# A hybrid decoder trunk: order of the first head's products, place of the residual-gate sums, evacuation of the delta gates

## The chip, the cores and the metric

The kernel runs on one core of a Trainium2 chip. The time is that of one execution on the device, in microseconds. A core has TensorE (PE, and PEld for its weight loads), VectorE (DVE), ScalarE (ACT), GpSimd (POOL) and SyncE (SP, whose queue here issues nearly all DMAs). Each works through its own queue in order and waits on semaphores of the others.

## The reference

One layer, sequence 1024, width 1024, float32:

```
shift, scale, gate = split(silu(c) @ ada_w + ada_b, 3)
h = rms_norm(x, norm_g) * (1 + scale) + shift
sq, sk, sv, sz, dq, dk, dv, dz, db, da, lq, lk, lv, lz, lr, mg = split(h @ w_in)
y_sb  = stick_breaking_attention(norm(q), norm(k), v) * silu(sz)      # 4 heads of 128
beta  = sigmoid(db);  g = -exp(a_log) * softplus(da + dt_bias)        # delta gates
y_gdn = rms_norm(gated_delta_rule(conv_silu(dq, dk, dv), beta, g)) * silu(dz)
y_gla = rms_norm(gla(lq, lk, lv, log_sigmoid(lr @ w2 + b) / 16)) * silu(lz)
merged = sum over the branches of sigmoid(mg) * (y_branch @ proj_branch)
out = x + gate * (merged @ w_out)                                     # residual gate
```

## The kernel before

Everything is kept transposed: channels on the 128 partitions, the 1024 tokens along a row. A float32 product is made of three: an operand is split into a high half (hi, rounded to fp32r) and the rest (lo), and hi x hi, hi x lo and lo x hi add up in one PSUM bank. `split` does it for a weight with a ScalarE cast (L157) and a VectorE subtraction (L158).

TensorE's instructions run in the order in which the program writes them. The other engines' instructions are put in order when the program is built, by a planner with its own estimates of time and with program order as priority. Tile pools give out a fixed number of buffers for each tag: 16 for "h" (the tiles of h and, at first, of ada), 8 for "raw" (weights as loaded), two PSUM banks for "acc", one for "tr".

**First head.** x is loaded, c is broadcast to all partitions and put through silu (`c_row`), and `rstd` comes out of sums of squares on TensorE. `keep_busy(5)` issues five products that nobody reads. Then a loop over the eight k tiles of h forms each tile and at once multiplies it with the first head's dq, dk, dv and dz weights. Four outputs (g) times two halves of the tokens (hf) take all eight PSUM banks, and a k tile makes 24 products. For each tile, `by_rows` (L374, L376) forms shift and scale: 128 rows of the transposed ada weight times `c_row`, summed along the row by VectorE, for the two of them. amp (L398) is (1 + scale) * norm_g; VectorE scales x with amp and rstd (L403), ScalarE adds shift and rounds to `hi` (L406), VectorE forms `lo` (L408). The loads of ada run three tiles ahead (`AHEAD`). Before, the 24 products go bank by bank:

```
for g in range(4):
    for hf in range(2):
        for n, (a, r) in enumerate(((0, hi), (0, lo), (1, hi))):
            mm(f_ps[g][hf], w[:, a, g, :], r[:, sl], 216, ...)
```

**Small projection and gates.** Then one group of 48 products (`run_cm`, two halves of 24, an acc bank each) projects lr, db and da together: rows 0 to 15, 32 to 35 and 64 to 67 of the output. `small_evac` copies it out with ScalarE (L503), GpSimd copies db (L504) and adds dt_bias to da (L505), and the lr rows go to DRAM. ScalarE forms sigmoid(db) (L515) and softplus(da) (L517 to L519), VectorE finishes and makes running sums by chunk (L520 to L526). The task `gates` (from L534) transposes these rows on TensorE into the one tr bank, four chunks at a time, and VectorE copies the bank into `beta_c` and `gam_c` (L542, L543); the second half needs the bank again.

**The rest.** `emit` writes TensorE's order by hand: it keeps a clock of planned matmul time (216 ns for a 512-wide product), and a task runs when its requirements are done and its lag in ns has passed; otherwise the next six products of the dense work (projections of later heads and merge gates, `run_cm`) are written. `gates` starts with a `yield 20400`. The tasks are the gated delta rule by head and half (G.a, G.b, G.v, G.s), GLA (L.w, L.p, L.s), attention (S.m) and, at the end of GLA, T.y, which loads y tiles into raw buffers and writes their differences. The task "cond" forms the residual gate: eight loads of 512 KB into the tags u6 and eight sums on VectorE (L314 to L318). Attention (`sb_mix`) runs roughly from 890 to 1150 us, merge and output projections after it. D.S2 is the end of the dense groups of the third attention head. The residual gate is read by the output projections alone.

Of the kernel before, what the change touches and what calls it, by code (L numbers as in the profile page):

```python
# [19 lines left out]
P = 128  # L20
D = 1024
# [31 lines left out]
def kernel(ctx: ExitStack, tc: tile.TileContext, xT: bass.AP, c: bass.AP,  # L53
# [258 lines left out]
    def conditioning(j, t_w="u6", t_p="u3"):  # L312
        aw = big(t_w)
        nc.sync.dma_start(out=aw, in_=adaT[j * P:(j + 1) * P, :])  # L314
        junk = big(t_p)
        nc.vector.tensor_tensor_reduce(out=junk, in0=aw, in1=c_row, scale=1.0, scalar=0.0,
                                       op0=ALU.mult, op1=ALU.add, accum_out=mod[:, j:j + 1])
        nc.vector.tensor_add(out=mod[:, j:j + 1], in0=mod[:, j:j + 1], in1=C("ada_b", j))  # L318
# [39 lines left out]
    keep_busy(5)  # L358
    AHEAD = 3

    def both(ap, k):
        return ap[:, k:k + 9:8]

    def conditioning2(k):
        tiles = [hp.tile([P, T], F32, tag="h", name="ada") for _ in range(2)]
        for i, t in enumerate(tiles):
            j = 8 * i + k
            nc.sync.dma_start(out=t, in_=adaT[j * P:(j + 1) * P, :])
        return lambda: by_rows(k, tiles)

    def by_rows(k, tiles):
        for i, t in enumerate(tiles):
            j = 8 * i + k
            nc.vector.tensor_tensor_reduce(out=t, in0=t, in1=c_row, scale=1.0, scalar=0.0,  # L374
                                           op0=ALU.mult, op1=ALU.add, accum_out=mod[:, j:j + 1])
        nc.vector.tensor_add(out=both(mod, k), in0=both(mod, k), in1=both(C("ada_b", 0, 24), k))  # L376


    first = (O_DQ, O_DK, O_DV, O_DZ)
    f_ps = [[None, None] for _ in first]  # L380
# [9 lines left out]
    for k in range(AHEAD):  # L390
        conds.append(conditioning2(k))
        if k < 3:
            raws.append(load_first(k))
    for k in range(KT):
        conds[k]()
        w = w_tile()
        split(w[:, 0], w[:, 1], raws[k])
        nc.vector.scalar_tensor_tensor(out=amp[:, k:k + 1], in0=mod[:, 8 + k:9 + k], scalar=1.0,  # L398
                                       in1=C("norm_g", k), op0=ALU.add, op1=ALU.mult)
        hi = hp.tile([P, T], F32R, tag="h", name="h_hi")  # L400
        lo = hp.tile([P, T], F32R, tag="h", name="h_lo")
        for sl in halves if k == 0 else (slice(0, T),):
# [4 lines left out]
                                 bias=mod[:, k:k + 1])  # L407
            nc.vector.scalar_tensor_tensor(out=lo[:, sl], in0=xs[k][:, sl],  # L408
# [9 lines left out]
        for g in range(4):  # L418
            for hf in range(2):
                if k == 0:  # L420
                    pool, tag = f_banks[2 * g + hf]
                    f_ps[g][hf] = bank(pool, tag, HALF)
                sl = slice(hf * HALF, (hf + 1) * HALF)
                for n, (a, r) in enumerate(((0, hi), (0, lo), (1, hi))):
# [74 lines left out]
    gt = [big("u7") for _ in range(2)]  # L499

    def small_evac(hf, sl, ps):
        raw = mid("v0")
        nc.scalar.copy(out=raw[0:96, :], in_=ps[0:96, :])  # L503
        nc.gpsimd.tensor_copy(out=rows[DB, sl], in_=raw[DB, :])  # L504
        nc.gpsimd.tensor_scalar(out=gt[0][DA, sl], in0=raw[DA, :], scalar1=C("dt_bias")[DA, :],  # L505
                                scalar2=None, op0=ALU.add)
        parts = [mid("v3", dt=F32R)[0:RANK, :] for _ in range(2)]
        split(*parts, raw[0:RANK, :])
# [5 lines left out]
    nc.scalar.activation(out=na[DA, :], in_=C("a_log")[DA, :], func=AF.Exp)  # L514
    nc.scalar.activation(out=rows[DB, :], in_=rows[DB, :], func=AF.Sigmoid)  # L515
    xg, sg = gt
    nc.scalar.activation(out=sg[DA, :], in_=xg[DA, :], func=AF.Abs)  # L517
    nc.scalar.activation(out=sg[DA, :], in_=sg[DA, :], func=AF.Exp, scale=-1.0)
    nc.scalar.activation(out=sg[DA, :], in_=sg[DA, :], func=AF.Ln, bias=one_c[DA, :])  # L519
# [1094 lines left out]
```

## Time and profile before

| | us |
|---|---|
| median of 3 runs | 1485.38 (1483.48 to 1486.11) |
| profiled execution | 1483.78 |
| its span | 1482.0 |

The span runs from the first to the last instruction that the profile shows; the rest of the execution's time lies around it. Times in the rows below are from the start of the span. An "idle before" is put down to the event that came last.

### The profile page before, as it was taken

The page shows a single profiled execution, that of the slowest core. Times are in us where ns is not written, and L with a number is a line of the kernel's source. Part 1 is how long each engine was busy: PE and PEld are TensorE (multiplying, and loading weights), DVE is VectorE, ACT ScalarE, POOL GpSimd, SP SyncE. Part 2 cuts the span into 40 slices and gives each one's busy share as a digit, 9 for nine tenths or more (in the row PEclk, how much of TensorE's full clock was granted, in tenths as well). Part 3 has the DMA queues.
Part 4 walks back from the last instruction along what each step waited for, and adds up shares of the span by engine and source line. Part 5 has one row for each costly group of instructions (what it writes and reads, how often), then busy time and mean ns, then how long its engine had stood idle before and what let it go on. Part 6 is the DMA issues. An engine that isn't in the chain of part 4 may idle for free.

```text
span 1482.0 us, 26690 instructions
## 1 busy us (share of the span) xinstructions
PE 1441.9 (97%) x10480; PEld 1206.6 (81%) x10480; DVE 918.8 (62%) x1914; ACT 697.9 (47%) x1470; POOL 151.5 (10%) x296
## 2 busy tenths in 40 slices
PE   7999999989999999999999999999999999999998
PEld 4877777877778887979788999899988888878777
DVE  7978647476643756667666535665566326589874
ACT  5367654453733747566486524342444434342321
POOL 1032232132321000000000100010000000000000
PEclk9999999999999999999999999999999999999999
DMA  9624332131321112121212132314223425474351
GB/s 351 183 78 118 102 88 62 44 92 42 104 86 40 41 51 66 35 60 35 73 47 54 55 107 72 100 43 147 60 86 108 142 85 171 139 244 129 119 175 61
DMA packets 174567, 144.31 MB, mean 97 GB/s; under 512 B 24773, under 2 KB 140613, under 8 KB 174442
## 3 DMA queue, kind: packets, MB, share of 16 engines
q1 hardware_dynamic: 174298, 142.30, 32.3%
q8 instruction: 82, 1.34, 0.4%
q14 instruction: 43, 0.35, 0.1%
q10 hardware_dynamic: 144, 0.31, 0.1%
HBM read 110.28 MB, written 32.29 MB: 96 GB/s over the span
## 4 chain that ended last, share of the span: by engine, by line
PE 76%; DVE 12%; DMA 4%; ACT 3%; POOL 2%; issue 2%; SPq 0%; DVEq 0%; POOLq 0%; ACTq 0%
PE acc L95 62%; PE lv L95 5%; PE mx L95 5%; PE tr L122 2%; DVE w L158 2%; DVE w L625 1%; DVE ada L374 1%; DVE w L623 1%; DVE u L435 1%; DMA v<-gam_d 1%; POOL c L301 1%; POOL u L505 1%; DVE u L403 1%; DVE h_lo L408 0%; ACT w L157 0%
## 5 line engine op out<-in xcount | busy, mean ns | idle before, releaser
L95 PE MATMUL acc<-h_hi,w 128*128 128x512 f32 x1856 | 653.4, 407 | 2.4 <-ACT u L295 2.0
L95 PEld LDWEIGHTS acc<-h_hi,w 128*128 128x128 f32 x1856 | 350.3, 189 | 73.8 <-ACT u L295 2.8
L95 PE MATMUL acc<-h_lo,w 128*128 128x512 f32 x928 | 364.1, 392 | 3.0 <-DVE h_lo L408 3.0
L157 ACT CAST w<-raw 128x512 fp32r<-128x512 f32 x232 | 141.8, 620 | 220.3 <-PE acc L95 192.0
L158 DVE TENSOR_TENSOR w<-raw,w 128x512 fp32r<-128x512 f32 x232 | 158.6, 691 | 129.4 <-ACT w L157 126.8
L95 PE MATMUL acc<-w,h_hi 128*128 128x256 f32 x1280 | 238.8, 287 | 0.0
L95 PEld LDWEIGHTS acc<-h_lo,w 128*128 128x128 f32 x928 | 175.9, 190 | 29.9 <-DVE h_lo L408 3.3
L95 PEld LDWEIGHTS acc<-w,h_hi 128*128 128x128 f32 x1280 | 198.8, 191 | 1.5 <-issue 0.7
L95 PE MATMUL acc<-w,h_lo 128*128 128x256 f32 x640 | 180.8, 282 | 0.0
L95 PE MATMUL acc<-u,w 128*128 128x512 f32 x744 | 180.0, 394 | 0.5 <-DVE v L1420 0.5
L95 PEld LDWEIGHTS acc<-u,w 128*128 128x128 f32 x744 | 139.5, 188 | 33.1 <-DVE v L1420 0.9
L95 PEld LDWEIGHTS acc<-w,h_lo 128*128 128x128 f32 x640 | 122.2, 191 | 0.0
L301 POOL TENSOR_TENSOR c<-c,mhalf 128x4 f32<-128x4 f32 (+1 forms) x56 | 54.9, 981 | 600.1 <-DVE c L299 575.7
L95 PE MATMUL acc<-unit,w 128*128 128x512 f32 x312 | 79.8, 393 | 1.1 <-DVE v L1475 1.1
L1224 ACT ACTIVATE v<-acc,col 128x512 f32<-128x512 f32 x48 | 33.0, 687 | 83.9 <-PE acc L95 83.4
L95 PEld LDWEIGHTS acc<-unit,w 128*128 128x128 f32 x312 | 58.4, 188 | 14.8 <-DVE v L1475 1.5
L1167 DVE TENSOR_TENSOR_SCAN u<-u,zero_c 128x128 f32<-128x128 f32 (+7 forms) x32 | 43.4, 1357 | 35.4 <-ACT u L1165 35.4
L95 PEld LDWEIGHTS mx<-r,u 128*128 128x128 f32 x288 | 44.2, 190 | 19.2 <-DVE r L804 5.2
L95 PE MATMUL mx<-r,u 128*128 128x128 f32 x288 | 48.3, 280 | 7.7 <-DVE r L804 2.8
L95 PE MATMUL lv<-u,u 128*32 128x32 f32 (+5 forms) x528 | 48.7, 250 | 2.2 <-DVE u L706 2.1
L95 PEld LDWEIGHTS lv<-u,u 128*32 128x32 f32 (+2 forms) x528 | 40.1, 145 | 11.2 <-issue 6.7
L295 ACT COPY u<-acc 128x512 f32<-128x512 f32 x50 | 29.1, 582 | 40.2 <-PE acc L95 39.6
(273 smaller groups left out, 1984.6 us busy)
## 6 DMA issues: line engine op xcount, KB each, us to landing
raw<-in_w_in SPq DMA_DIRECT2D x160, 256.0 KB, 3.1
g_dram<-v SPq DMA_DIRECT2D x48, 256.0 KB, 2.1
v<-g_dram SPq DMA_DIRECT2D x48, 256.0 KB, 2.9
ada<-in_adaT SPq DMA_DIRECT2D x16, 512.0 KB, 8.7
u<-in_xT SPq DMA_DIRECT2D x8, 512.0 KB, 7.6
u<-in_adaT SPq DMA_DIRECT2D x8, 512.0 KB, 3.7
v<-gam_d SPq DMA_DIRECT2D x16, 256.0 KB, 3.3
y_dram<-v SPq DMA_DIRECT2D x16, 256.0 KB, 2.1
```

The costliest lines, as they stand in the source:

```text
L95: return nc.tensor.matmul(out, lhsT=lhsT, rhs=rhs, **kw)
L122: nc.tensor.transpose(out=out, in_=in_, identity=ident[:k, :k])
L157: nc.scalar.copy(out=hi, in_=raw)
L158: nc.vector.tensor_sub(out=lo, in0=raw, in1=hi.bitcast(F32))
L295: nc.scalar.copy(out=dst[:, sl], in_=ps)
L301: nc.gpsimd.tensor_tensor(out=out, in0=out, in1=mhalf[:, 0:n], op=ALU.pow)
L374: nc.vector.tensor_tensor_reduce(out=t, in0=t, in1=c_row, scale=1.0, scalar=0.0, op0=ALU.mult, op1=ALU.add, accum_out=mod[:, j:j + 1])
L403: nc.vector.scalar_tensor_tensor(out=xs[k][:, sl], in0=xs[k][:, sl], scalar=amp[:, k:k + 1], in1=rstd[:, sl], op0=ALU.mult, op1=ALU.mult)
L435: nc.vector.scalar_tensor_tensor(out=t, in0=r[:, tap:tap + T], scalar=C("conv", j + tap), in1=t, op0=ALU.mult, op1=ALU.add)
L505: nc.gpsimd.tensor_scalar(out=gt[0][DA, sl], in0=raw[DA, :], scalar1=C("dt_bias")[DA, :], scalar2=None, op0=ALU.add)
L1167: nc.vector.tensor_tensor_scan(om[:, 0:n][:, ::-1], om[:, 0:n][:, ::-1], zero_c.broadcast_to([P, n]), 1.0, ALU.mult, ALU.add)
L1224: nc.scalar.activation(out=g, in_=ps, func=AF.Identity, bias=C("merge_b", gi * 8 + d))
```

## The change

- First head: for each k tile the 24 products run in the order high weight x hi (eight products, four outputs for each half of the tokens), low weight x hi (eight), high weight x lo (eight). `hi` of both halves is formed ahead of `lo`. One more warming product.
- The sums of k tiles 0 and 1 are formed together, ahead of amp for both; from then on one tile at a time. ada of tile 1 is loaded ahead of the first w tile. amp is formed in `by_rows`.
- c is written to DRAM once (4 KB). The task "cond" goes; a task T.c with the requirement D.S2 forms the residual gate in half rows: a broadcast of half of c into a raw buffer, eight loads of 256 KB into raw buffers and eight half sums, twice, 2500 ns of planned time between the steps. G.a no longer requires "cond", which had a lag of 1000 behind `gates`.
- Gates: ScalarE's evacuation adds dt_bias to all 96 rows (it is zero outside 64 to 67) and writes straight into `xg`; the two GpSimd instructions go, and sigmoid moves behind the softplus.

```diff
+    c_dram = dp.tile([1, T], F32, name="c_dram")
+    nc.sync.dma_start(out=c_dram, in_=c_row[0:1, :])
+
+    def gate_cond():
+        sums = cp.tile([P, 2, 8], F32, name="sums")
+        for hf, sl in enumerate(halves):
+            cr = flat(raw_tile())
+            nc.sync.dma_start(out=cr, in_=c_dram[:, sl].broadcast_to([P, HALF]))
+            for j in range(8):
+                aw = flat(raw_tile())
+                nc.sync.dma_start(out=aw, in_=adaT[(16 + j) * P:(17 + j) * P, sl])
+                yield 2500
+                nc.vector.tensor_tensor_reduce(out=aw, in0=aw, in1=cr, scale=1.0, scalar=0.0,
+                                               op0=ALU.mult, op1=ALU.add,
+                                               accum_out=sums[:, hf, j:j + 1])
+        nc.vector.tensor_add(out=sums[:, 0], in0=sums[:, 0], in1=sums[:, 1])
+        nc.vector.tensor_add(out=mod[:, 16:24], in0=sums[:, 0], in1=C("ada_b", 16, 8))
...
-    keep_busy(5)
+    keep_busy(6)
...
+    def by_rows(k0, n=1):
+        ks = slice(k0, k0 + n)
+        for k in range(k0, k0 + n):
+            for i, t in enumerate(conds[k]):
...
+        nc.vector.tensor_add(out=mod3[:, 0:2, ks], in0=mod3[:, 0:2, ks], in1=bias3[:, 0:2, ks])
+        nc.vector.scalar_tensor_tensor(out=amp[:, ks], in0=mod3[:, 1, ks], scalar=1.0,
+                                       in1=C("norm_g", k0, n), op0=ALU.add, op1=ALU.mult)
...
         conds.append(conditioning2(k))
-        if k < 3:
+        if k == 1:
+            raws.append(load_first(0))
+        if k:
             raws.append(load_first(k))
     for k in range(KT):
-        conds[k]()
+        if k != 1:
+            by_rows(k, 2 if k == 0 else 1)
...
-        for g in range(4):
-            for hf in range(2):
...
-                for n, (a, r) in enumerate(((0, hi), (0, lo), (1, hi))):
+        for n, (a, r) in enumerate(((0, hi), (1, hi), (0, lo))):
+            for hf, sl in enumerate(halves):
+                for g in range(4):
                     mm(f_ps[g][hf], w[:, a, g, :], r[:, sl], 216,
...
     def small_evac(hf, sl, ps):
-        raw = mid("v0")
-        nc.scalar.copy(out=raw[0:96, :], in_=ps[0:96, :])
-        nc.gpsimd.tensor_copy(out=rows[DB, sl], in_=raw[DB, :])
-        nc.gpsimd.tensor_scalar(out=gt[0][DA, sl], in0=raw[DA, :], scalar1=C("dt_bias")[DA, :],
-                                scalar2=None, op0=ALU.add)
+        nc.scalar.activation(out=xg[0:96, sl], in_=ps[0:96, :], func=AF.Identity,
+                             bias=C("dt_bias")[0:96, :])
...
-    tasks = [("gates", gates, [], 0), ("cond", gate_cond, ["gates"], 1000)]
+    tasks = [("gates", gates, [], 0)]
...
-                      ["gates", "cond", f"D.G{h}"] + prev(n, 1, "G.a") + prev(n, 3, "G.s"), 3000))
+                      ["gates", f"D.G{h}"] + prev(n, 1, "G.a") + prev(n, 3, "G.s"), 3000))
...
+    tasks.append(("T.c", gate_cond, ["D.S2"], 0))
```

## Rows read from the trace of the kernel before

**Rows 1.** Page, part 1: busy us, share of the span, instructions
```profile
PE 1441.9 (97%) x10480; PEld 1206.6 (81%) x10480; DVE 918.8 (62%) x1914; ACT 697.9 (47%) x1470; POOL 151.5 (10%) x296
```

**Rows 2.** The waits of TensorE, whole span: us in total, times, longest us
```profile
PE tr L122 <- DVE gam_c L543: 3.9, 1, 3.9
...
PE acc L95 <- DVE h_lo L408: 3.0, 1, 3.0
...
PE acc L95 <- ACT u L295: 2.0, 2, 1.6
```

**Rows 3.** Timeline of TensorE, 0 to 125 (start us, us, what, [idle before, releaser])
```profile
18.92 4.45 PE L95 MATMUL tr<-cst,ones 128*128 128x512 f32 x10
...
27.24 0.79 PE L95 MATMUL acc<-h_lo,w 128*128 128x512 f32 x1 [2.97 <-DVE h_lo L408]
...
35.25 0.39 PE L95 MATMUL acc<-h_hi,w 128*128 128x512 f32 x1
...
40.69 0.39 PE L95 MATMUL acc<-h_hi,w 128*128 128x512 f32 x1
...
73.33 0.39 PE L95 MATMUL acc<-h_hi,w 128*128 128x512 f32 x1
```

**Rows 4.** Timeline of VectorE, 14 to 62
```profile
17.18 1.22 DVE L374 CUSTOM_DVE_ANT_0 ada<-ada,u 128x1024 f32<-128x1024 f32 x1
...
22.21 0.75 DVE L403 SCALAR_TENSOR_TENSOR u<-u,amp,u 128x512 f32<-128x512 f32 x1 [2.28 <-ACT u L354]
...
40.51 1.29 DVE L403 SCALAR_TENSOR_TENSOR u<-u,amp,u 128x1024 f32<-128x1024 f32 x1
...
51.36 1.28 DVE L403 SCALAR_TENSOR_TENSOR u<-u,amp,u 128x1024 f32<-128x1024 f32 x1
```

**Rows 5.** Timeline of ScalarE, 60 to 145: the last h_hi
```profile
63.22 1.15 ACT L406 ACTIVATE h_hi<-u,mod 128x1024 fp32r<-128x1024 f32 x1
```

**Rows 6.** Timeline of GpSimd, 60 to 145
```profile
80.69 10.16 POOL L505 TENSOR_SCALAR u<-v,col 4x512 f32<-4x512 f32 x1
```

**Rows 7.** Timeline of ScalarE, 60 to 145: behind the gate rows
```profile
91.71 1.06 ACT L515 ACTIVATE u<-u 4x1024 f32<-4x1024 f32 x1 [4.38 <-POOL u L504]
92.79 1.28 ACT L442 ACT_TABLE_LOAD   x1
94.09 1.06 ACT L442 ACTIVATE u<-u 128x1024 f32<-128x1024 f32 x1
```

**Rows 8.** Timeline of VectorE, 60 to 145
```profile
106.55 2.62 DVE L526 TENSOR_TENSOR_SCAN u<-ones,u 4x128 f32<-4x128 f32 x8
...
112.20 1.22 DVE L316 CUSTOM_DVE_ANT_0 u<-u,u 128x1024 f32<-128x1024 f32 x1
...
114.02 0.17 DVE L542 COPY beta_c<-tr 128x16 f32<-128x16 f32 x1
```

**Rows 9.** Timeline of TensorE, 83 to 150
```profile
96.89 0.50 PE L95 MATMUL acc<-h_hi,w 128*128 128x512 f32 x1 [1.63 <-ACT u L295]
...
114.41 0.68 PE L122 MATMUL tr<-cst,u 128*128 128x128 f32 x4 [3.85 <-DVE gam_c L543]
114.80 0.73 PE L95 MATMUL acc<-h_hi,w 128*128 128x512 f32 x1
...
118.30 0.62 PE L95 MATMUL acc<-h_hi,w 128*128 128x512 f32 x2
```

**Rows 10.** Stretches of 10 us: busy us of each engine, granted clock, DMA share
```profile
90.00:100.00 10.00, 8.37 (x38) 6.59 (x37) 1.52 (x4) 8.14 (x9) 3.22 (x5) 1.00 0.47 129
```

**Rows 11.** Timeline of SP's DMA issues, 0 to 150
```profile
10.19 1.61 SPq L368 DMA_DIRECT2D ada<-in_adaT  x2
```

**Rows 12.** The tile ada: its loads from issue to landing
```profile
DMA to landing us min/median/max: 4.5/8.7/10.7
```

**Rows 13.** Stretches of 50 us: busy us of each engine
```profile
1000.00:1050.00 50.00, 50.00 (x360) 46.29 (x360) 26.39 (x37) 15.52 (x32) 0.00 (x0) 1.00 0.46 138
```

**Rows 14.** The page's DMA issues: KB each, median us to landing
```profile
raw<-in_w_in SPq DMA_DIRECT2D x160, 256.0 KB, 3.1
```

More of the change, by code (lines that the diff above doesn't have):

```diff
@@ L368, in conditioning2 @@
             nc.sync.dma_start(out=t, in_=adaT[j * P:(j + 1) * P, :])
[L369 to L380, printed above, removed]
+        return tiles
+    mod3, bias3 = (t.rearrange("p (i k) -> p i k", i=3) for t in (mod, C("ada_b", 0, 24)))
+    def by_rows(k0, n=1):
+        ks = slice(k0, k0 + n)
+        for k in range(k0, k0 + n):
+            for i, t in enumerate(conds[k]):
+                j = 8 * i + k
+                nc.vector.tensor_tensor_reduce(out=t, in0=t, in1=c_row, scale=1.0, scalar=0.0,
+                                               op0=ALU.mult, op1=ALU.add,
+                                               accum_out=mod[:, j:j + 1])
+        nc.vector.tensor_add(out=mod3[:, 0:2, ks], in0=mod3[:, 0:2, ks], in1=bias3[:, 0:2, ks])
+        nc.vector.scalar_tensor_tensor(out=amp[:, ks], in0=mod3[:, 1, ks], scalar=1.0,
+                                       in1=C("norm_g", k0, n), op0=ALU.add, op1=ALU.mult)
     f_banks = ((pa, "acc"), (pa, "acc"), (pm, "mx"), (pm, "mx"), (pt, "tr"), (pl, "lv"),
@@ L407 @@
                                  bias=mod[:, k:k + 1])
+        for sl in parts:
             nc.vector.scalar_tensor_tensor(out=lo[:, sl], in0=xs[k][:, sl],
@@ L417 @@
         h_lo.append(lo)
-        for g in range(4):
-            for hf in range(2):
[L420 to L423, printed above, removed]
-                for n, (a, r) in enumerate(((0, hi), (0, lo), (1, hi))):
+        if k == 0:
+            f_ps = [[bank(*f_banks[2 * g + hf], HALF) for hf in range(2)] for g in range(4)]
+        for n, (a, r) in enumerate(((0, hi), (1, hi), (0, lo))):
+            for hf, sl in enumerate(halves):
+                for g in range(4):
                     mm(f_ps[g][hf], w[:, a, g, :], r[:, sl], 216,
@@ L498 @@
     nc.gpsimd.memset(rows, 0.0)
-    gt = [big("u7") for _ in range(2)]
+    xg, sg = (big("u7") for _ in range(2))
     def small_evac(hf, sl, ps):
-        raw = mid("v0")
-        nc.scalar.copy(out=raw[0:96, :], in_=ps[0:96, :])
-        nc.gpsimd.tensor_copy(out=rows[DB, sl], in_=raw[DB, :])
-        nc.gpsimd.tensor_scalar(out=gt[0][DA, sl], in0=raw[DA, :], scalar1=C("dt_bias")[DA, :],
-                                scalar2=None, op0=ALU.add)
+        nc.scalar.activation(out=xg[0:96, sl], in_=ps[0:96, :], func=AF.Identity,
+                             bias=C("dt_bias")[0:96, :])
         parts = [mid("v3", dt=F32R)[0:RANK, :] for _ in range(2)]
-        split(*parts, raw[0:RANK, :])
+        split(*parts, xg[0:RANK, sl])
         for i, n in enumerate((0, 1, 0)):
@@ L513 @@
         pass
-    nc.scalar.activation(out=na[DA, :], in_=C("a_log")[DA, :], func=AF.Exp)
-    nc.scalar.activation(out=rows[DB, :], in_=rows[DB, :], func=AF.Sigmoid)
-    xg, sg = gt
     nc.scalar.activation(out=sg[DA, :], in_=xg[DA, :], func=AF.Abs)
     nc.scalar.activation(out=sg[DA, :], in_=sg[DA, :], func=AF.Exp, scale=-1.0)
+    nc.scalar.activation(out=na[DA, :], in_=C("a_log")[DA, :], func=AF.Exp)
     nc.scalar.activation(out=sg[DA, :], in_=sg[DA, :], func=AF.Ln, bias=one_c[DA, :])
+    nc.scalar.activation(out=rows[DB, :], in_=xg[DB, :], func=AF.Sigmoid)
     nc.vector.scalar_tensor_tensor(out=sg[DA, :], in0=xg[DA, :], scalar=0.0, in1=sg[DA, :],
@@ L1529 @@
                       [f"G.v{key}"] + prev(n, 1, "G.s"), 1050))
-    for n, (h, q) in enumerate(halves):
+    for n, (h, q) in enumerate(parts):
         g, key = L[h], f"{h}.{q}"
```

25 lines of the change are left out of this document (5 added, 20 removed).

## The prediction

> **What bounds the kernel now.** I read the busy shares first: TensorE is busy for 97% of the span [rows 1], so time comes back only where it idles or runs at its lower clock. The waits of TensorE rank the idling [rows 2]: the longest is the second transpose of the gate rows waiting for the copy into gam_c (3.9 us), then the first low product of the first head (3.0), and the two evacuations of an acc bank (2.0). All three lie in the first 120 us, which is where the change works. So the timeline of TensorE comes next, then those of the engines that it waits for.
>
> In the first head [rows 3], five warming products end at 18.92 + 4.45 = 23.37. One product follows, and then TensorE stands 2.97 us for h_lo of the first k tile. Once settled, a k tile takes 40.69 - 35.25 = 5.44 us for 24 products, 0.227 each. The small projection begins at 73.33. From 27.24 there are 191 products left, 43.3 us at the settled pace, and 46.1 passed: the other 2.8 us are products just after the wait at half the pace, the lower of the clock's two levels. VectorE is the close second: from one scaling of x to the one two tiles on, 51.36 - 40.51 = 10.85 us pass, 5.43 a tile [rows 4], with no idle between. It stood still only before 22.21, for 2.28 us, when the sums of tile 0 were done and rstd was not. The last h_hi starts at 63.22 and takes 1.15 [rows 5].
>
> The gates come next. GpSimd takes 10.16 us to add dt_bias to four rows [rows 6]. ScalarE, whose queue is in order, stands 4.38 us behind it with the sigmoid, then changes table at 1.28 us, and the evacuations queue behind [rows 7]; TensorE pays 1.63 us at 96.89 and the rest of the 2.0 at the next bank. The same lateness pushes the gate arithmetic on VectorE among the convolutions and the residual-gate sums: such a sum runs at 112.20, the copy of beta only at 114.02 [rows 8]. That holds the one tr bank, and TensorE stands 3.85 us until 114.41 [rows 9]. The eight products from 114.80 to 118.30 then take 3.5 us where 1.8 would do, half the pace again: 1.7 us more. In the ten microseconds that hold the 1.63 us gap the granted clock was 1.00 [rows 10], so a gap of that size cost its own length alone.
>
> **The change, part by part.** *High half first.* Of 24 products of a tile, 16 now need only h_hi, so h_lo may come 16 x 0.227 = 3.6 us after it. In the first tile h_lo came 2.97 us late, so the wait goes and, with it, the fall of the clock. The sixth warming product (0.89, from 4.45 / 5) ends at 24.3, and the first h_hi is there by then, since the one early product had ended at 27.24 - 2.97 = 24.27; it hides the start of the loop, and costs what the first product then begins late. 24.3 + 192 x 0.227 = 67.8, against 73.33: 5.5 us.
>
> *Sums of two tiles at once.* Four sums of 1.22 us from 17.18 end at 22.1, inside the 2.28 us that VectorE stood before rstd, so tile 1's two sums are free. Everything behind comes 2.3 us earlier; the last h_hi is ready near 63.22 + 1.15 - 2.3 = 62.1, and 5.44 us of products end at 67.5. The two bounds, 67.8 by TensorE and 67.5 by VectorE, meet, which is also the danger: neither has room. The sums need tile 1's rows of ada. They are now issued ahead of the first w tile; before they were issued from 10.19 to 11.80 [rows 11], and the slowest load of ada took 10.7 us [rows 12], so they might land at 22.5, the last sum end at 23.7 and amp be 1.8 us late. The ends are 3.7 and 5.5. The median landing of 8.7 is nearer to the good one; I take 5.0. The 4 KB write of c to DRAM stands in SP's queue, which would hold the loads behind it until c_row exists; xT still fills the queues then (SP is far ahead of what lands), so nothing.
>
> *One evacuation for the gates.* Adding dt_bias in ScalarE's evacuation removes two GpSimd copies and two additions, 10.16 us of them one after another on the chain. ScalarE then runs Abs, Exp, Ln and Sigmoid back to back, each 1.06 with a table change of 1.28: at most 4 x 2.34 = 9.4 us, and TensorE needs an acc bank again only 48 products (10.9 us) after the small projection. So the 2.0 us of bank waits go; the ends are 0 and 2.0, and I take 2.0. The gate rows are then ready some 14.5 us after the small projection (9.4, then VectorE's scans, 2.62, behind two steps of four rows that I estimate at the 1.22 of a sum), while the order written out for TensorE brings the transposes after 20.4. They were in time before too; what was late was the copy out of the bank. With the gate arithmetic earlier and the residual-gate sums gone from this stretch, VectorE has little ahead of the copies. I leave one convolution step of about the length of a sum (1.2) in the way in most outcomes. A gap as short as that did not lower the clock at 96.89. So of 3.85 + 1.7 = 5.5 us I take 4.5; the ends are 0 and 5.5.
> In the trace a table change is 1.28 us and the next instruction starts at 94.09, 0.02 us after its end [rows 7]. The Trainium skill (ScalarE: Activation LUTs, What ACT_TABLE_LOAD costs) has a drain of about 1.38 us on top. By it the chain would take an estimated 5.5 us more and use up nearly all the slack before the transposes; by the rows it doesn't.
>
> *Gate preparation starts 1 us sooner.* Without the task "cond" the first gdn_prep comes one step of six products (1.4 us) earlier, and all recurrences shift against the dense work. No row prices this: bounds -3 and +3, the size of the longest single waits [rows 2]; I take 0.
>
> *Residual-gate sums moved.* Eight loads of 512 KB and eight sums leave the stretch before 120. Into the attention stage go sixteen half sums, two broadcasts and sixteen loads of 256 KB through SP's queue. A half sum is about 0.6 us (half of 1.22), 10 us in all. From 1000 to 1050 TensorE is busy throughout, and VectorE 26.39 of 50 [rows 13]; it would rise to about 36. The cover is that slack; if it were gone, each half sum ahead of a weight split or a copy that feeds TensorE would cost 0.6. Bounds 0 and 5 (half of them); I take 0.5.
>
> **Sum.** 5.0 + 2.0 + 4.5 - 0.5 = 11.0 us. The profiled execution took 1483.78, span 1482.0 and 1.78 around it, which gives 1472.8. The median of the runs, 1485.38, lies 1.6 above it and would give 1474.4. I say 1474.
>
> **Rivals.** *The copies still come late.* VectorE's order is made when the program is built; if G.q's convolution again stands ahead of the copies, the 3.85 and 1.7 stay: 11.0 - 4.5 = 6.5 us, 1479. For it: the convolution steps are already interleaved with them. Against: they were there because the gate arithmetic came after 10 us of GpSimd.
>
> *VectorE or the loads set the first head.* If a k tile's h_hi is late by a sum (1.2) once or twice, 2.5 us of the 5.0 are lost: 1476.5. For it: 5.43 against 5.44.
>
> *Weight buffers run out in the attention stage.* This is the one that ends slower. The eight raw buffers now also hold a broadcast row and one or two ada pieces for sixteen steps of 2.5 us, some 40 us, during which about four weight groups of 10.9 us pass. If the next group's load has to queue behind an ada piece, TensorE waits out a whole landing, 3.1 us [rows 14], and 1.7 more at the lower clock: 4.8 each. From three groups on (14.4) it eats the gain; four (19.2) make 1493. For it: SP fills the buffers in order, and a piece is freed only when VectorE has summed it. Against: no TensorE wait at all in that stretch now.
>
> *Changing banks.* Each product now goes to another bank than the one before. The present kernel changes bank every third product and the pitch stays 0.227. If a change of bank made TensorE stutter until its clock fell for half of the 192 products, 96 x 0.22 = 21 us would be lost: 1495. It decides from 50 such products on (11 / 0.22).
> The Trainium skill (TensorE: Matmul & The Clock Gate, A second HAM failure mode: psum-queue depth-cycling) tells of such a kernel, cycling through banks with its clock swinging between its levels. The trace so far speaks against it.
>
> *It shifts and gives nothing.* The earlier recurrences meet new waits worth the whole gain: 1484. It would take four of the longest.
>
> **Chances.** Forecast 0.60, late copies 0.17, first head short 0.12, weight buffers 0.04, banks 0.03, nothing 0.04. About 0.2% (3 us) is what can be told from no change here. Forecast, late copies and short head are faster: 0.89. "Nothing" and a little of the buffers are the same: 0.05; the rest is slower: 0.06. The forecast's own range is 1469 (from 1483.78, every term at its good end and 2 from the shift) to 1477 (from 1485.38, the first head at 3.7 and 1.3 less elsewhere); an end at 1480.5 takes in both smaller gains, so 1469 to 1480.5 leaves out under 2 in 10.
>
> **What would show it.** Right: products from 24.3 on without a gap and at the high clock, the small projection starting near 68; no addition by GpSimd; no wait of TensorE for L295 near 90; the second gate transpose following the first at once near 102, without products at half pace; no wait of TensorE between 990 and 1060. Wrong: a gap before the second tile's first product, the copy of gam_c behind convolution steps, SP waiting on a raw buffer while TensorE waits for a split.

## The result, and the profile after

The changed kernel is slower: 1492.94 us median of four runs (1492.36 to 1496.05) against 1485.46 for the kernel before on the same chip, a ratio of 1.0056 to it (its 95% interval, here and below, in brackets: [1.0042, 1.007]). The forecast was 1474, with 1480.5 as its upper end, so it had the wrong sign. The profiled span is 1490.6, against 1482.0. One execution of single_sums below took 1747.11 us at a granted clock of 0.754 and isn't counted.

Part 1 of the page after, and its waits of TensorE over the whole span (us in total, times, longest), which answer to [rows 1, 2]:

```profile
PE 1446.5 (97%) x10482; PEld 1208.7 (81%) x10482; DVE 915.9 (61%) x1922; ACT 701.0 (47%) x1473; POOL 137.6 (9%) x292
```

```profile
PE mx L95 <- POOL u L784: 6.2, 2, 4.0
...
PE lv L95 <- ACT w L682: 3.1, 2, 2.3
...
PE tr L122 <- DVE u L1180: 2.3, 1, 2.3
...
PE acc L95 <- DVE v L1431: 1.8, 1, 1.8
...
PE tr L122 <- DVE gam_c L554: 1.5, 2, 0.8
```

The shares alone would say that little happened. The waits say that what was aimed at did go: no line of `h_lo`, none of the evacuation L295, and 1.5 us for gam_c in place of 3.9. Near the head of the list stand waits that belong to the gated delta stage (L784, L682) and to attention (L1180), where the change was not meant to act. (Lines after are those of before plus 11 from about L500 on: L784 was L773, L1240 was L1229.)

Where the time went is read by one comparison, used from here on: both kernels copy the same acc banks out of PSUM in the same order, so the start of the same copy in either trace tells how far one is ahead of the other. The copies taken are those at 79, 113, 199, 236, 336, 432, 914, 1006, 1057 and 1414 us of before. In the table, minus is earlier than before, in us:

| profiled run | 79 | 113 | 199 | 236 | 336 | 432 | 914 | 1006 | 1057 | 1414 |
|---|---|---|---|---|---|---|---|---|---|---|
| the change | -3.0 | -7.9 | -9.8 | -6.6 | -5.1 | -0.7 | -1.1 | -0.5 | 5.4 | 8.4 |

So up to 199 us the change earned 9.8 us, where the prediction's terms up to there make 11.5. The delta stage took 9 of them back by 432, attention cost 6 more between 1006 and 1057, and the merge the last 3. The merge's part is the wait for L1431 in the list above: VectorE, timeline 1316 to 1332, stood for the load of a merge gate (`g_dram`).

```profile
1321.76 0.69 DVE L1431 TENSOR_TENSOR v<-v,acc 128x512 f32<-128x512 f32 x1 [1.84 <-DMA v<-g_dram]
```

TensorE waited 1.76 us behind it (0.52 before), and its products from 1323.33 to 1326.31 were 0.43 apart, at half the pace. In no other profile is this wait longer than 0.95; whether it comes back in other executions of the change isn't shown.

**First head.** TensorE's timeline after, 18 to 72, and under it ScalarE's and VectorE's of the first 28 us (start, us, what, idle before), for [rows 3, 4]:

```profile
19.82 5.31 PE L95 MATMUL tr<-cst,ones 128*128 128x512 f32 x12
25.79 0.50 PE L95 MATMUL acc<-h_hi,w 128*128 128x512 f32 x1 [0.65 <-ACT h_hi L422]
...
43.14 0.50 PE L95 MATMUL acc<-h_hi,w 128*128 128x512 f32 x1 [0.73 <-ACT h_hi L422]
...
70.47 0.39 PE L95 MATMUL acc<-h_hi,w 128*128 128x512 f32 x1
```

```profile
25.01 1.39 ACT L422 ACTIVATE h_hi<-u,mod 128x512 fp32r<-128x512 f32 x2 [0.90 <-DVE u L419]
```

```profile
23.62 0.69 DVE L158 TENSOR_TENSOR w<-raw,w 128x512 fp32r<-128x512 f32 x1 [1.01 <-ACT w L157]
24.23 1.41 DVE L419 SCALAR_TENSOR_TENSOR u<-u,amp,u 128x512 f32<-128x512 f32 x2
```

The 2.97 us before the second product is gone, the clock stays at 1.00 (window 20 to 60), and the pitch is 0.227 with a change of bank at each product. The first product comes at 25.79, not 24.3: the warming products start at 19.82 where they started at 18.92 (x landed later in this execution, VectorE's first step on it starting at 8.01 for 7.65, as it did in a kernel that is the same as before up to there, see the end; the rest of the 0.9 wasn't followed), and VectorE, which had stood before rstd, now does the low half of the first weights ahead of the scaling of x. The small projection starts at 70.47 against 73.33.

**Gates.** TensorE's timeline, 94 to 125, for [rows 9]:

```profile
103.13 0.60 PE L122 MATMUL tr<-cst,u 128*128 128x128 f32 x4
105.94 0.63 PE L122 MATMUL tr<-cst,u 128*128 128x128 f32 x4 [0.83 <-DVE gam_c L554]
111.35 0.63 PE L122 MATMUL tr<-cst,u 128*128 128x128 f32 x4 [0.67 <-DVE gam_c L554]
```

Two waits of under 1 us in place of one of 3.85, and the products behind them keep the full pace.

**Delta stage.** The longest wait of the run, after: TensorE's timeline at 204 to 216, then ScalarE's and GpSimd's just ahead of it.

```profile
209.07 0.80 PE L95 MATMUL mx<-r,u 128*128 128x128 f32 x2 [4.02 <-POOL u L784]
209.51 0.77 PE L95 MATMUL acc<-h_hi,w 128*128 128x512 f32 x1
210.09 0.63 PE L95 MATMUL acc<-h_lo,w 128*128 128x512 f32 x1
```

```profile
201.61 1.28 ACT L1240 ACT_TABLE_LOAD   x1
202.90 0.63 ACT L1240 ACTIVATE v<-v 128x512 f32<-128x512 f32 x1
...
204.58 1.28 ACT L780 ACT_TABLE_LOAD   x1
205.88 1.28 ACT L780 ACTIVATE v<-v,gneg_c 128x128 f32<-128x128 f32 x4
207.06 0.61 ACT L783 ACTIVATE v<-v 128x512 f32<-128x512 f32 x1
```

```profile
207.75 1.26 POOL L784 TENSOR_TENSOR u<-u,v 128x512 f32<-128x512 f32 x1 [1.85 <-ACT v L783]
```

And the same places in the trace of before, ScalarE and then TensorE:

```profile
214.95 0.63 ACT L772 ACTIVATE v<-v 128x512 f32<-128x512 f32 x1
215.66 1.28 ACT L769 ACTIVATE v<-v,gneg_c 128x128 f32<-128x128 f32 x4
```

```profile
218.12 0.49 PE L95 MATMUL mx<-r,u 128*128 128x128 f32 x2 [2.11 <-POOL u L773]
...
218.69 0.40 PE L95 MATMUL acc<-h_lo,w 128*128 128x512 f32 x1
218.92 0.63 PE L95 MATMUL acc<-h_hi,w 128*128 128x512 f32 x2
```

TensorE needs `qd` (the line writes `mx`), GpSimd makes it from exp(gb), and ScalarE makes that. Before, ScalarE did exp(gb) first and the four other exps behind it. After, a sigmoid of a merge gate (L1240) stands between two groups of exps and costs two table changes of 1.28, and exp(gb) comes last. The wait grows from 2.11 to 4.02 us, and only behind the longer one do the products run 0.43 to 0.58 apart, at half the pace; the clock of the stretch says the same:

```profile
205.00:215.00 10.00, 5.98 (x22) 4.95 (x21) 6.12 (x21) 4.38 (x10) 3.43 (x4) 0.66 0.24 66
...
1000.00:1050.00 50.00, 47.03 (x334) 43.48 (x334) 31.00 (x58) 12.77 (x27) 0.00 (x0) 0.97 0.60 190
```

The last line is the attention stretch and answers to [rows 13]: 47.03 us of TensorE for 50.00.

### The profile page after: what moved, and what is told of

The parts are those of the page before. It is cut to its first block, busy times and chain, and to the rows that moved or that the text cites. A ratio compares the mean times of both kernels' runs of the same rounds, so it can differ in the third digit from the quotient of the medians.

```text
span 1490.6 us, 26720 instructions
## 1 busy us (share of the span) xinstructions
PE 1446.5 (97%) x10482; PEld 1208.7 (81%) x10482; DVE 915.9 (61%) x1922; ACT 701.0 (47%) x1473; POOL 137.6 (9%) x292
## 4 chain that ended last, share of the span: by engine, by line
PE 73%; DVE 10%; DMA 6%; ACT 5%; issue 2%; POOL 2%; SPq 1%; DVEq 0%; POOLq 0%; ACTq 0%
PE acc L95 60%; PE mx L95 6%; PE lv L95 5%; PE tr L122 2%; DVE u L450 2%; DVE w L158 1%; DMA v<-gam_d 1%; POOL c L301 1%; DMA raw<-in_adaT 1%; DVE w L634 1%; DVE w L636 1%; DMA u<-in_xT 1%; DMA u<-y_dram 1%; DMA raw<-y_dram 1%; ACT w L157 1%
## 5 line engine op out<-in xcount | busy, mean ns | idle before, releaser
L95 PEld LDWEIGHTS acc<-unit,w 128*128 128x128 f32 x312 | 58.4, 188 | 15.2 <-DVE v L1486 1.5
L295 ACT COPY u<-acc 128x512 f32<-128x512 f32 x50 | 29.1, 582 | 37.1 <-PE acc L95 36.9
```

The source lines that it names most:

```text
L95: return nc.tensor.matmul(out, lhsT=lhsT, rhs=rhs, **kw)
L295: nc.scalar.copy(out=dst[:, sl], in_=ps)
```

## The experiments

Theories for the delta stage. *Shift*: the gate preparation starts one step sooner and runs into work that isn't ready. *Queues*: the planner draws the orders of VectorE, ScalarE and GpSimd anew, and the draw of before was a good one. In the first expectations any new build does that; from lag_longer on, only moving the gate preparation, either way, does. *Chain*: the early gains are lost anyway. For attention: *Buffers* (the loads of the residual gate stand in SP's queue for raw buffers) against *VectorE* (the half sums themselves). The kernel before had a median between 1483.97 and 1486.83 on the chips used, so each kernel is told with its ratio to before on its own chip. The same copies as above, in the profiled runs (one execution each):

| profiled run | 79 | 113 | 199 | 236 | 336 | 432 | 914 | 1006 | 1057 | 1414 |
|---|---|---|---|---|---|---|---|---|---|---|
| lag_kept | -3.6 | -8.5 | -9.4 | -10.2 | -8.0 | -8.4 | -8.8 | -7.9 | -1.4 | -1.7 |
| sums_early | -2.7 | -7.0 | -6.9 | -7.5 | -7.9 | -8.4 | -8.7 | -8.1 | -7.1 | -6.8 |
| sums_late_alone | 2.0 | -0.9 | -3.1 | -3.9 | -1.2 | -1.5 | -1.9 | -1.6 | 4.5 | 5.0 |
| lag_alone | 0.9 | 0.9 | 4.0 | 6.5 | 9.2 | 12.5 | 12.1 | 12.4 | 12.4 | 12.9 |
| first_head_alone | -2.9 | -3.5 | 1.1 | 2.0 | 0.4 | 0.4 | 0.0 | 0.2 | 0.2 | 0.1 |
| gates_alone | 1.1 | -3.9 | -5.9 | -6.6 | -7.7 | -8.0 | -8.4 | -8.1 | -8.1 | -8.1 |
| sums_in_gla | -2.8 | -7.7 | -8.7 | -9.5 | -9.9 | -9.9 | -8.5 | -8.1 | -8.1 | -7.5 |
| sums_in_gla_again | -2.7 | -7.6 | -8.3 | -7.6 | -7.6 | -7.4 | -6.0 | -5.7 | -5.8 | -5.5 |
| lag_longer | -3.0 | -7.9 | -3.0 | -4.1 | 6.2 | 3.5 | 3.8 | 4.3 | 4.5 | 4.0 |
| lag_two_longer | -2.6 | -7.3 | -3.7 | -5.5 | 3.5 | 1.5 | 1.8 | 2.2 | 2.2 | 2.5 |
| single_sums | -1.8 | -5.3 | -2.5 | -3.3 | -5.0 | -4.6 | -4.9 | -4.4 | -3.6 | -3.3 |
| sums_own_buffers | 5.6 | 1.7 | 5.0 | 4.2 | 6.5 | 6.2 | 5.8 | 6.1 | 6.1 | 5.7 |
| loads_without_sums | -3.1 | -8.0 | -9.3 | -10.0 | -8.5 | -8.5 | -8.9 | -8.2 | 0.4 | -0.1 |
| sums_without_loads | -3.4 | -8.3 | -9.3 | -10.0 | -11.5 | -11.8 | -12.1 | -11.5 | -8.3 | -8.3 |

The two rows of sums_in_gla are one kernel, and differ by up to 2.5 us; so a difference of that size between two rows is not read as the work of an edit.

**lag_kept** puts the lag back by an empty task that does nothing:

```diff
+    def nothing():
+        return
+        yield
-    tasks = [("gates", gates, [], 0)]
+    tasks = [("gates", gates, [], 0), ("cond", nothing, ["gates"], 1000)]
-                      ["gates", f"D.G{h}"] + prev(n, 1, "G.a") + ...
+                      ["gates", "cond", f"D.G{h}"] + prev(n, 1, "G.a") + ...
```

> The changed kernel with an empty task in the place of cond, so that the first gdn_prep keeps its old lag and TensorE's order after the first head is that of the kernel before. Theory Shift (the one step by which gdn_prep moved forward costs the 9 us that the changed kernel gives back between 200 and 480 us): the lead of about 10 us at 199 us is still there at 480, the attention stage then takes its 6 us and the merge 2.7, about 1484. Theory Queues (the other engines' orders, planned anew at every build, cost it): part of the lead is lost although TensorE's order is the old one, 1486 to 1491. Theory Chain (the recurrences are bound by their own latency and cannot start earlier with profit): all of the lead is lost by 480, about 1493 as in the changed kernel.

Measured: 1480.09 us, ratio 0.9974 [0.9964, 0.9985]. From 113 to 432 the lead goes from -8.5 to -8.4, where that of the change fell from -7.9 to -0.7: the loss of the delta stage hangs on that one step. No theory had this time: Shift said 1484, Queues 1486 and more, and Queues in its first form falls, since a new build kept the lead. Most of the lead then goes in attention, from -7.9 to -1.4.

**sums_early** has the first head and the gates of the change, and the task "cond" with its eight whole sums as before.

```diff
-    tasks = [("gates", gates, [], 0)]
+    tasks = [("gates", gates, [], 0), ("cond", gate_cond, ["gates"], 1000)]
...
-    tasks.append(("T.c", gate_cond, ["D.S2"], 0))
```

> The changed kernel with the residual-gate sums back in their old place and form, task cond included; first head and gates as changed. Shift: 1475 (the lead of 10 us kept to the end). Queues: some of the lead lost in the recurrence stage, 1476 to 1482, with waits on other lines than in the changed kernel. Chain: 1485, no gain. All three: no loss of 5 us between 1030 and 1060 us, since no gate sum stands there.

Measured: 1479.32 us, ratio 0.997 [0.996, 0.998], and 1.0 us lost in attention.

**sums_late_alone** is the kernel before with the empty task and T.c as in the change.

> The kernel before with only the residual-gate sums moved into the attention stage; an empty task keeps the lag of gdn_prep, so TensorE's order is that of before throughout. Theory Buffers (the half sums take raw buffers and SP's queue, and the weight loads come late): the time line is level with before up to 1030 us, loses 4 to 6 us by 1060, with TensorE idle and its clock down between 1040 and 1050; about 1490, up to 1493 if the merge loses too. Rival, VectorE alone (the 16 half sums delay its other work a little each): 1 to 2 us, 1487, and the weight loads are in time.

Measured: 1485.10 us, ratio 1.001 [0.9999, 1.0021]. It gains about 4 us where the sums left (from 2.0 at 79 to -1.9 at 914) and loses 6.1 where they went.

**lag_alone** is the kernel before with one word taken out:

```diff
-                      ["gates", "cond", f"D.G{h}"] + prev(n, 1, "G.a") + ...
+                      ["gates", f"D.G{h}"] + prev(n, 1, "G.a") + ...
```

> The kernel before with gdn_prep no longer behind cond (one name taken out of one list); cond itself stays. Shift: 5 to 9 us slower, 1490 to 1494, lost between 200 and 480 us. Queues: anything from 3 us faster to 4 us slower, 1482 to 1489. Chain: no change, 1485.

Measured: 1497.07 us, ratio 1.0089 [1.0074, 1.0104], 13.1 us above before, nearly all of it lost between 113 and 432. That is more than any theory said; Shift, with 5 to 9, is nearest. Its waits of TensorE from 120 to 440 us begin with the one for qd, 4.0 us long as in the changed kernel; the second, one line below, is 1.4 there:

```profile
PE mx L95 <- POOL u L773: 6.3, 2, 4.0
PE lv L95 <- POOL w L649: 5.2, 2, 3.7
```

Set side by side with the trace of before, place by place (source line, operation, tile names and shapes; table loads and accumulator reads left out), lag_alone has another instruction in 1284 of TensorE's 10480 places, 315 of VectorE's 1890, 88 of ScalarE's 1191 and 21 of GpSimd's 296, all between 120 and 417 us. In lag_kept and sums_early the orders of TensorE, ScalarE and GpSimd between 140 and 436 us are those of before; VectorE's differs in one instruction of 549 and in three.

**lag_longer** and **lag_two_longer** are sums_early with the first gate preparation one and two steps later than before, which Shift and Queues answer differently. Against sums_early:

```diff
-    tasks = [("gates", gates, [], 0), ("cond", gate_cond, ["gates"], 1000)]
+    tasks = [("gates", gates, [], 0), ("cond", gate_cond, ["gates"], 2300)]
```

(3600 in the second.)

> First head and gates of the change, residual-gate sums in their old place, but the first gate preparation one step of six products LATER than before (lag 2300 for 1000), where the change has it one step earlier. Theory Queues: each step, whichever way, makes the planner draw VectorE's, ScalarE's and GpSimd's order in the delta stage anew, and the order of the kernel before is a lucky one; the draw costs some 5 to 12 us: median 1485 to 1491, with new waits of TensorE for GpSimd or ScalarE between 150 and 400. Rival Shift: only an earlier start is bad, because the recurrences then run into work that isn't ready; a later start costs at most its own 1.4 us: median 1479 to 1481.

> First head and gates of the change, residual-gate sums in their old place, the first gate preparation two steps later than before (lag 3600 for 1000). Theory Queues: a third draw of the orders in the delta stage; the lead of 7 to 8 us at 120 is lost again by 5 us or more before 430, median 1482 to 1492. Rival: one step either way was bad luck twice, and a draw is on average neutral: median 1477 to 1481.

Measured: 1488.87 us, ratio 1.0022 [1.0009, 1.0035], and 1484.6 us, 0.9994 [0.9982, 1.0006]. Both arrive at 113 with the lead of sums_early (-7.9 and -7.3) and lose 11.4 and 8.8 us of it by 432. Their own delay is 1.4 and 2.8. By the medians, against that of sums_early, they cost 9.1 and 3.6. Shift falls: later is bad too. Each draw has long waits of its own, again behind engines that are fed in a new order; the first line of each list:

```profile
PE lv L95 <- DVE w L676: 6.0, 3, 2.9
```

```profile
PE lv L95 <- DVE u L706: 4.8, 1, 4.8
```

But waiting is mostly the smaller part of the loss. Below is the stretch between the copies at 113 and 432 of before, in each kernel's own trace: before, the change, lag_alone, lag_longer, lag_two_longer (busy us of TensorE, its weight loads, VectorE, ScalarE and GpSimd, then the granted clock).

```profile
113.00:432.00 319.00, 301.98 (x2467) 243.23 (x2468) 202.22 (x614) 176.44 (x433) 92.29 (x188) 0.99 0.30 82
...
105.00:431.00 326.00, 304.68 (x2465) 244.43 (x2465) 197.09 (x606) 180.14 (x435) 90.58 (x187) 0.98 0.28 78
...
114.00:444.00 330.00, 308.66 (x2463) 247.44 (x2464) 200.38 (x614) 180.33 (x435) 91.69 (x188) 0.97 0.29 79
...
105.00:435.00 330.00, 308.52 (x2459) 247.25 (x2459) 201.16 (x615) 178.67 (x434) 89.79 (x188) 0.96 0.30 81
...
106.00:433.00 327.00, 308.75 (x2458) 247.93 (x2459) 200.09 (x615) 180.92 (x436) 91.22 (x188) 0.96 0.30 82
```

TensorE idles 17.0 us before and 18.3 to 21.5 in the four others; for the same products it is busy 2.7, 6.7, 6.5 and 6.8 us longer, as the granted clock falls. So in the last three most of the loss is products at half the pace, not waiting. (One execution each; the two profiles of sums_in_gla have a clock of 1.00 and 0.99 in this stretch.)

**first_head_alone** and **gates_alone** are the kernel before with one of the two groups of edits each.

> The kernel before with the first head's edits alone: order of the products, sums of tiles 0 and 1 together, sixth warming product. Theory Additive: the first head ends 2.9 us earlier, as in the changed kernel, and TensorE's later order is that of before, so the lead lasts: median about 3 us under the kernel before (2 to 4). The evacuation of the gates still goes over GpSimd, so the bank waits (2.0) and the late copy of gam_c (3.9) are there. Rival Chain: the gate rows set when the delta stage can run and GpSimd's 10 us are still in them; then the lead is used up by 130 us and the median is within 1 us of before. Rival Redrawn: moving VectorE's first instructions redraws its later order too and costs some microseconds, median 0 to 10 above before.

> The kernel before with the gates' edits alone: ScalarE's evacuation adds dt_bias, no GpSimd instructions, sigmoid last. TensorE's order is untouched. Theory Additive: first head and gates together led by 7 us, the first head by 2.9 of it; so the gates alone lead by about 4 us from 120 us on (bank waits 2.0 gone, wait for gam_c 3.9 down to about 1.5), median 3 to 5 under before. Rival: the copies are late because VectorE has the residual-gate sums and convolutions ahead of them; then only the bank waits go, median 1 to 2 under before.

Measured: 1483.66 us, ratio 0.999 [0.9977, 1.0003], and 1478.02 us, 0.9954 [0.9937, 0.9972]. Additive fails: the gates alone give all of it, the first head nothing that can be told from none. The first head's 3.5 us at 113 are gone at 199. In its trace, TensorE (first fence) and VectorE (second), and under them TensorE at the same place before:

```profile
168.25 1.08 PE L95 MATMUL lv<-u,u 64*64 64x64 f32 x8 [3.18 <-DVE u L710]
169.26 0.79 PE L95 MATMUL acc<-h_hi,w 128*128 128x512 f32 x1
```

```profile
163.02 0.17 DVE L627 TENSOR_TENSOR w<-w,w 32x15 f32<-32x15 f32 x1 [2.93 <-DMA w<-ad]
```

```profile
170.00 0.65 PE L95 MATMUL lv<-u,u 64*64 64x64 f32 x8 [0.96 <-DVE u L706]
```

TensorE got to this step of the inverse 4 us sooner. It waits for VectorE's copies L710 (L706 before), and ahead of those, in VectorE's in-order queue, stand steps of a gate preparation (L627) whose rows come back from DRAM (`ad`) only 2.2 us sooner than before. So TensorE waits 3.18 for 0.96 and runs at half pace behind it. That the recurrence doesn't come sooner with the dense products is what Chain said, with the loss some 50 us later than it put it. In gates_alone the recurrence moves and the lead grows from -3.9 to -8.0.

**single_sums** is sums_early with the first two tiles' sums one at a time again.

> First head and gates of the change, residual-gate sums in their old place, but the sums of k tiles 0 and 1 one tile at a time as before. Theory Pair sums matter: with single sums the first tile is ready 1.2 us sooner, yet VectorE is then 2.4 us behind for the later tiles and sets the first head: waits for h_hi between 30 and 70 and the small projection no sooner, median 0 to 2 above the kernel with pair sums (1479 to 1481). Rival: the pair sums only delay the first product (amp at 22.5, first product at 25.8 for 24.3 forecast); then single sums gain 1 us.

Measured: 1478.6 us (the four executions counted), ratio 0.9955 [0.9937, 0.9973]. The small projection is about 1 us later than with pair sums (-1.8 for -2.7), and at the end the two can't be told apart: one more sign that time won in the first head doesn't reach the end.

For attention, ScalarE, SP's issues and TensorE of lag_kept:

```profile
1031.72 0.62 ACT L1329 CAST u<-u 128x512 fp32r<-128x512 f32 x1 [4.32 <-DMA u<-y_dram]
...
1034.81 0.28 ACT L1176 ACTIVATE u<-lv 128x128 f32<-128x128 f32 x1
```

```profile
1027.02 0.33 SPq L323 DMA_DIRECT2D raw<-in_adaT  x1
...
1028.04 0.38 SPq L1328 DMA_DIRECT2D u<-y_dram  x1
```

```profile
1036.87 0.33 PE L122 MATMUL tr<-cst,u 128*128 128x128 f32 x1 [2.21 <-DVE u L1180]
1036.95 0.63 PE L95 MATMUL acc<-h_hi,w 128*128 128x512 f32 x1
1037.38 0.63 PE L95 MATMUL acc<-h_lo,w 128*128 128x512 f32 x1
```

and its list of SP's waits between 1000 and 1060:

```profile
SPq L323 <- DVE sums L325: 11.4, 8, 3.6
```

SP stands 11.4 us, in eight waits, until a half sum has given a raw buffer back for the next piece of ada. Behind it in the queue is a load of y_dram; ScalarE, in order, stands 4.32 us behind that load's cast, and behind the cast are the sigmoids (L1176) of the third attention head (an expectation below calls it the fourth). The scan and its product (L1180) follow on VectorE, from 1036.00 on, behind weight splits and a half sum at 1034.19; TensorE waits 2.21 us, and its next products are 0.43 apart.

**sums_own_buffers** is lag_kept with two buffers of their own and GpSimd's queue for the pieces (and for the two broadcasts).

```diff
-                aw = flat(raw_tile())
-                nc.sync.dma_start(out=aw, in_=adaT[...])
+                aw = wp.tile([P, HALF], F32, tag="own", name="own", bufs=2)
+                nc.gpsimd.dma_start(out=aw, in_=adaT[...])
```

> The changed kernel with the old lag kept and the residual-gate sums in attention as the change has them, but their tiles from two buffers of their own and their loads issued by GpSimd's queue. The half sums on VectorE stay where they were. Theory Queue of SP: nothing is then ahead of the y_dram loads and the weights in SP's queue, ScalarE's 4.32 us stand behind such a load goes, and the wait of 2.2 for the first transposes of the fourth head (L122) with it; attention costs under 1.5 us, median 7 to 9 under before (about 1476). Rival VectorE: the half sums themselves hold the scans and copies of attention; the 2.2 us wait and the half-pace products stay, and the median is 3 to 5 under before, as with the raw buffers.

Measured: 1489.55 us, ratio 1.0024 [1.0011, 1.0036], for another reason: with nothing to hold them, the planner spread the half sums from 23 to 158 us, two of them in the first head, where TensorE waited 7.7 us for one h_hi. It doesn't test what it was made for, since no half sum ran in attention.

**loads_without_sums** and **sums_without_loads** part the two, on lag_kept. The first sums 8 of 512 columns of each piece; the second does not load the pieces and multiplies constants in their place. Neither forms the residual gate.

```diff
-                nc.vector.tensor_tensor_reduce(out=aw, in0=aw, in1=cr, ...
+                nc.vector.tensor_tensor_reduce(out=aw[:, 0:8], in0=aw[:, 0:8], in1=cr[:, 0:8], ...
```

```diff
-                nc.sync.dma_start(out=aw, in_=adaT[(16 + j) * P:(17 + j) * P, sl])
-                nc.vector.tensor_tensor_reduce(out=aw, in0=aw, in1=cr, ...
+                nc.vector.tensor_tensor_reduce(out=aw, in0=cst[:, 0:HALF], in1=cr, ...
```

> The version with the old lag kept, residual-gate sums in attention, but each half sum over 8 of its 512 columns (so the residual gate is wrong); broadcasts and the sixteen loads of 256 KB stay. Theory Queue of SP: the loads are what costs; a load of y_dram still comes late, ScalarE stands 2 us or more behind it near 1030, and the lead that the profile has at 998 falls by 4 us or more to 1060. Rival VectorE: with the half sums gone the lead falls by less than 2 us.

> The same version, but the sixteen pieces of ada are not loaded: each half sum multiplies a half row of the constants with the broadcast of c and writes it into the raw buffer (so the residual gate is wrong); buffers and half sums stay, only two broadcasts are loaded. Theory Queue of SP: without the loads SP holds nothing back for long; the lead at 998 falls by less than 2 us to 1060. Rival VectorE: sixteen half sums of 0.69 us hold the scans and copies of attention; the lead falls by 4 us or more.

Measured: 1483.23 us, ratio 0.998 [0.997, 0.999], and 1478.38 us, 0.9949 [0.9931, 0.9967]. From 1006 to 1057 the first loses 8.6 us, the second 3.2, lag_kept 6.5. The first line of TensorE's waits from 990 to 1070, with loads and without:

```profile
PE tr L122 <- DVE u L1180: 4.5, 1, 4.5
```

```profile
PE tr L122 <- DVE u L1179: 2.5, 1, 2.5
```

The loads are the larger part, as Buffers said. But without them 3.2 us go too, more than the 2 expected: SP still stands 9.6 us for buffers that half sums hold (L175 behind L324), so this remainder may belong to the buffers or to VectorE, and isn't parted. Nor is the way from the loads to TensorE tested by an edit of its own: that the y_dram load is the link is read from lag_kept's rows.

**sums_in_gla** asks for the residual gate in the GLA stage, with the old lag:

```diff
-    tasks.append(("T.c", gate_cond, ["D.S2"], 0))
+    tasks.append(("T.c", gate_cond, ["D.Lq2"], 0))
```

> The changed kernel with the old lag of the gate preparation kept by an empty task, and the residual-gate sums asked for when the queries of the third GLA head are done (some 500 us in the run) instead of in attention. Theory Queue of SP: in attention the 5 to 7 us go because a load of y_dram stands in SP's queue behind ada pieces that wait for a raw buffer, and ScalarE, in order, stands 4.32 us behind that load with the sigmoids of the next attention head. In the GLA stage no such load is in the queue, so the sums cost under 1 us; the lead of 8.8 us that the kernel with the kept lag has at 998 lasts, median 8 to 9 under before (about 1475). Rival VectorE: sixteen half sums of 0.69 us, 11 us of VectorE, are in the way wherever they stand: the loss of 4 to 6 us shows up at their new place, median 3 to 5 under before (about 1480).

> The version with the residual-gate sums in the GLA stage and the old lag once more, with more rounds: median 6 to 9 us under before (ratio 0.994 to 0.996).

Measured: 1477.00 us, ratio 0.9942 [0.9922, 0.9963], and on another chip 1477.69 us, 0.9948 [0.9934, 0.9962]. This version beats both kernels, before by 7.4 and 7.9 us and the change by some 15. The sums cost 1.4 us where they now stand (-9.9 at 432, -8.5 at 914, and -7.4 and -6.0 in the second profile), and attention next to nothing. It is not told apart from gates_alone (0.9954).

## Why the prediction was wrong

The step that failed is "Gate preparation starts 1 us sooner", with bounds of -3 and +3 and 0 taken. lag_alone prices it at 13.1 us. The bound was worked out from the size of one wait of TensorE, as if only the recurrences moved against the dense products. And the list of waits was read as if its longest all lay in the first 120 us. Between the rows of [rows 2] stand others; from 120 to 440 us alone, in the trace of before, nine lines with 15.2 us, four of them above the 2.0 of the evacuations; the first two:

```profile
PE lv L95 <- POOL u L456: 2.6, 1, 2.6
PE mx L95 <- POOL u L773: 2.6, 2, 2.1
```

So the stage that the step would disturb was already one of small waits behind three engines, and it wasn't priced. What moved with the recurrences is the order of three other engines, which the planner makes from its own estimates of time, and the prediction said of it, in a rival about one copy, "VectorE's order is made when the program is built", without asking what else that order decides. Four draws (the change, lag_alone, one and two steps later) lost 7 to 12 us between 113 and 432. Of the kernels that keep the order, lag_kept, sums_early, sums_late_alone and gates_alone lost 0.1 or nothing, single_sums 0.7, and first_head_alone 3.9, its own gain. How a draw costs is followed in one place, the 4.02 us: a sigmoid among the exps, exp(gb) last. Whether the rest comes from the orders of ScalarE, VectorE and GpSimd or from TensorE's own moved steps was not parted; every draw changed both.

Point by point:
- *High half first, sums of two tiles* (5.0 taken, ends 3.7 and 5.5): by the profiled spans from the first warming product to the small projection, 73.33 - 18.92 = 54.41 before and 70.47 - 19.82 = 50.65 after, 3.8 us, the low end. Two waits, of 0.65 (behind VectorE's split of the first weights) and 0.73, took most of what is missing from the 5.5. But the term is worth nothing at the end: first_head_alone is at 0.999. The sum counted it whole, because it asked what TensorE waits for in the first head and not what the next stage waits for.
- *Evacuation* (2.0) and *late copies* (4.5): 6.5 together. gates_alone gains 6.4 by the medians; in its profile 5.0 is there by 113 us (from 1.1 to -3.9) and 4 more come in the delta stage. The mechanism was right, and this is the part that lasts. That 6.4 meets 6.5 is partly luck: the sum expected nothing of it in the delta stage.
- *Table change*: after, one ends at 202.89 and the next instruction starts at 202.90. The drain of about 1.38 us that the Trainium skill (ScalarE: Activation LUTs, What ACT_TABLE_LOAD costs) adds doesn't show here either.
- *Residual-gate sums* (0.5 taken, ends 0 and 5): 5.9 us between 1006 and 1057 in the changed kernel, against some 4 won where they left (sums_late_alone), which the sum didn't count; the 9.8 at 199 us, so near the forecast, hold some of them. The mechanism was that of the rival "weight buffers run out", SP standing behind buffers that ada holds, but it was priced at the weights. TensorE waited for none of them in that stretch; a load of y_dram came late, and behind it ScalarE's queue and the next head's sigmoids.
- *Changing banks*: no sign, 0.227 a product at a clock of 1.00; what the Trainium skill (TensorE: Matmul & The Clock Gate, A second HAM failure mode: psum-queue depth-cycling) tells of such a pattern isn't seen in this kernel.

Put together by medians: -4.7 (sums_early), +13.1 (lag_alone) and +1.1 (sums_late_alone) make +9.5, and +7.5 was measured. The sign and most of the size come from the one step.

## What to carry to other kernels

When a planner orders the queues, an edit to a dependency list can be an edit to all of them (here four of four cost time): price it as a new draw, or keep the old slot with an empty task and measure the edit by itself. Follow a gain to the stage behind it, and ask what sets that stage's pace; here time won ahead of the gates was lost where VectorE's queue stood behind a round trip through DRAM. For work that is moved into slack, look at what stands behind its loads in the in-order queue, not only at the busy share of the engine that computes it.

## What was not expected of the hardware

The pace behind a wait doesn't follow its length in these rows. After 2.11 us (the wait for qd, 218.12, before) the products went on 0.23 apart; after 2.21 (1036.87, lag_kept), 3.18 (168.25) and 4.02 (209.07) they were 0.43 or more apart for 3 to 6 us. But the same wait for qd was 1.95 in first_head_alone, with half the pace behind it (granted clock 0.50 from 219 to 221), and a later one for qd was 2.32 in lag_alone, with the full pace behind it (1.00 from 394 to 396):

```profile
219.00 0.80 PE L95 MATMUL mx<-r,u 128*128 128x128 f32 x2 [1.95 <-POOL u L777]
```

```profile
393.94 0.49 PE L95 MATMUL mx<-r,u 128*128 128x128 f32 x2 [2.32 <-POOL u L773]
```

So the length of a wait alone doesn't tell here which pace follows. Behind the 4.02 the half pace lasted until 214.2, some 4.7 us, and so lost about 2.3 more: a wait that grew by 1.9 cost 4.2.

The first warming product, up to which before and lag_alone are the same kernel, began at 18.92 in the one and 19.82 in the other (VectorE's first step on x at 7.65 and 8.04); in the others it began at 19.1 to 20.7. The 18.92 from which the prediction counted was an early one, and so the first columns of the tables show up to a microsecond less than was won there.
